# A two-block transformer kernel on one core: the modulation rows, x's first norm and the load order at its beginning

## The chip, the core and the metric

One core of a Trainium2 chip runs the whole program. Its engines are TensorE (PE in the rows, its weight loads PEld), VectorE (DVE), ScalarE (ACT) and GpSimd (POOL); SyncE (SP) issues nearly all loads. The metric is the device time of one execution in microseconds. The kernel before takes 1417.83 us (median of 3 runs, 1417.08 to 1421.2).

## The reference

The input is one sequence of 256 tokens, 1024 wide. Two layers with adaptive norms are followed by a third layer; each has several FFNs and mixers. What concerns the change is the very beginning, layer 0's first FFN, and the long filter that layer 1 needs:

```python
cond = jax.nn.silu(c)
m = (cond @ w_mod[l] + b_mod[l]).reshape(bsz, 3, 3, D_MODEL)      # 9 sections of 1024
def adaln_in(x, g, m, i):
    return rmsnorm(x, g) * (1 + m[:, i, 1][:, None]) + m[:, i, 0][:, None]
def swiglu(h, w1, w3, w2):
    return (jax.nn.silu(h @ w1) * (h @ w3)) @ w2                    # 2752 wide inside
x = x + 0.5 * m[:, 0, 2][:, None] * swiglu(adaln_in(x, norm_g[l, 0], m, 0), ...)

# hyena_filter: three sine layers on 33 features of 256 positions, then 64 -> 2 x 512
h = jnp.sin(fq * (z @ w1 + b1))     # three of these, then
h = (h @ w4).reshape(L, 2, CONV_WIDTH) * decay
```

So before FFN 0 can start, `silu(c)` must meet 1024 x 2048 numbers of `w_mod` (the scale section and the shift section), and x must be squared and summed.

## The kernel before, in words

Everything is kept transposed: features on the 128 partitions, the 256 tokens along the free axis. Each weight tile is 128 x 1024 in float32 (512 KB). ScalarE rounds it to a high part (`hi_job`, L584), VectorE subtracts to get the low part (`lo_job`, L595), and each product is three one-pass matmuls: high by high, high by low, low by high (`mm3`). An FFN's first half is 43 slabs of 8 such blocks, so 24 matmuls a slab; `slab_mms` (L678) takes the first three slabs together, and three PSUM tiles (`mmr`, `u_127` to `u_129` in the order) hold them. The second half follows in `block_mms`.

All loads go through one list (`order`, L549): `m` tiles of `w_mod`, `w` tiles of weights. SyncE issues them in that order into a ring of six raw tiles (`raws`, `u_75` to `u_80`); a tile comes free when its last reader has run, and an issue that waits holds up all behind it. `RATES` says how many `m` tiles follow each `w` tile; `extra` and `EX` put the small loads (x, the filter's tables, vectors) ahead of a given entry.

Modulation is made in two ways. An `m` tile of the usual kind holds 128 outputs on the partitions and 1024 inputs along the free axis: one VectorE multiply-and-sum (`tensor_tensor_reduce` against `condb`, the row `silu(c)` copied to all partitions) gives 128 outputs. For the groups of four tiles named in `PE_GROUPS` (L133) the tiles are stored the other way round and `pe_mod` (L630) makes 512 outputs as a row on TensorE: eight float32 matmuls with a one-column stationary operand `c` and 512 moving columns each, then a ScalarE copy and four small matmuls that turn the row into columns. Before, only group 2 goes this way. Groups 0 and 1 are the scale section, 2 and 3 the shift section.

FFN 0 is the only one whose norm is applied before its matmuls (`nm.whole`): ScalarE squares the eight blocks of x, GpSimd adds them, TensorE sums over partitions, VectorE makes the inverse root, `spread` makes a tile of it, and `normalise` (L818) multiplies x by the gain and by it, in one VectorE instruction a block, and splits the result. The shift is carried as two more columns of the operand (258 instead of 256, `shift_cols`), and comes back out of PSUM as a bias that ScalarE copies before each silu. Beside this `hyena_spectrum` (L1528) makes the filter; `reduce_angle` brings its angles into range with GpSimd and VectorE in turn; its last layer adds and subtracts the two halves of `w4` on GpSimd, `tap_sums` squares and adds on ScalarE and GpSimd.

The program is written by generators under a planner (`Sched`, L330): each job says which engine it wants next, and the one with the earliest modelled start plus a penalty is emitted. On the chip each engine then runs its list strictly in that order. All engine calls pass through one helper, so nearly every row of the profile has line L442.

Of the kernel before, what the change touches and what calls it, by code (L numbers as in the profile page):

```python
# [20 lines left out]
P = 128  # L21
# [111 lines left out]
PE_GROUPS = (2,)  # L133
# [4 lines left out]
def _pack(inp):  # L138
# [135 lines left out]
    out["fw4"] = np.ascontiguousarray(inp["d_f_w4"][0])  # L274
# [18 lines left out]
EX = (2, 3, 8)  # L293
DRATE, DLAT = 350.0, 1.3
HPEN = -0.6
# [5 lines left out]
RATES = [(43, 0.55), (65, 0.7), (91, 0.5), (156, 0.31), (199, 0.5), (221, 0.75), (247, 0.4), (10 ** 6, 0.2)]  # L301
# [28 lines left out]
class Sched:  # L330
# [61 lines left out]
    def charge(self, e, cost, early=0.0, cols=0.0):  # L392
# [19 lines left out]
        if e == "pe":  # L412
            self.debt = 0.0 if j.main else self.debt + cost

# [59 lines left out]
def _body(tc, ins, out, ctx, dbg=None):  # L474
# [74 lines left out]
    order = [("m", i) for i in range(12)] + [("w", 0)] + [("m", i) for i in range(12, 16)]  # L549
    mi, credit = 16, 0.0  # L550
    for i in range(NW):
        if i:
            order.append(("w", i))
# [8 lines left out]
    m_ev = {(l, s): Event() for l in range(2) for s in range(9)}  # L562
    cond_ev, x_ev = Event(), Event()
# [31 lines left out]
    def lo_job():  # L595
        for oi, (kind, i) in enumerate(order):
# [13 lines left out]
            else:  # L610
# [8 lines left out]
                mod_done(l, M_SECS[r // 8], 1)  # L619
# [4 lines left out]
    def mod_done(l, s, n):  # L624
        m_left[l, s] = m_left.get((l, s), 8) - n
        if m_left[l, s] == 0:
            fire(m_ev[l, s])


    def pe_mod(g, ccol, one1, row):  # L630
# [3 lines left out]
        for i in range(4):  # L634
            oi = order.index(("m", 4 * g + i))
            yield raw_ev[oi]
# [4 lines left out]
            put(raws, raw_t.pop(oi))  # L641
        yield "act"
        act.activation(row, b[0:1], AF.Copy)
# [3 lines left out]
        for j in range(4):  # L647
            pe.matmul(b[:, j:j + 1], row[:, j * P:j * P + P], one1[:, 0:1], start=True, stop=True)
# [3 lines left out]
        mod_done(0, M_SECS[g // 2], 4)  # L652
# [140 lines left out]
    class Norm:  # L793
        def __init__(self, A, h, lo, width=D):
# [5 lines left out]
            self.adder = ("dve", dve)  # L800
# [17 lines left out]
        def normalise(self, k, src):  # L818
            yield self.done
            t, = yield sc, 1  # L820
            yield "dve"
            dve.scalar_tensor_tensor(t, src, self.A[:, k:k + 1], self.rstd, ALU.mult, ALU.mult)
            yield from split(self.h[:, k, :T], self.lo[:, k, :T], t, self.need(k))
            put(sc, t)
            self.use()
# [7 lines left out]
        def square(self, src):  # L833
# [110 lines left out]
    def ffn(l, i, nm, nxt):  # L944
        with tc.tile_pool(name=f"ffn{l}{i}", bufs=1) as sp:
# [5 lines left out]

            def done(s, ps):
                t, = yield sc, 1
                b, = yield sm, 1
                if nm.whole:
                    h = ps[:, :T]
                    yield "act"
                    act.activation(b[:, 0:1], ps[:, T:T + 1], AF.Copy)
                else:
                    h = t  # L960
                    yield from evict(nm, t, b[:, 0:1], ps)
                j = s // 2
                if s == 42:
# [4 lines left out]
                    if nm.whole:  # L968
                        put(mmr, ps)
# [5 lines left out]
                elif s % 2 == 0:  # L975
                    yield "act"
                    act.activation(t, h, AF.Silu, bias=b[:, 0:1])
                    if nm.whole:
                        put(mmr, ps)
# [4 lines left out]
                else:  # L984
# [3 lines left out]
                    if nm.whole:  # L988
                        put(mmr, ps)
# [5 lines left out]
            if not nm.whole:  # L995
# [509 lines left out]
    def reduce_angle(a, shift):  # L1505
        t, = yield sc, 1
        n = t[:a.shape[0], :a.shape[1]]
        yield "pool"
        if shift:
            pool.tensor_scalar(n, a, 1.0 / TWO_PI, shift / TWO_PI, ALU.mult, ALU.add)  # L1510
            pool.tensor_scalar(n, n, MAGIC, None, ALU.add)
        else:
            pool.tensor_scalar(n, a, 1.0 / TWO_PI, MAGIC, ALU.mult, ALU.add)
        yield "pool"
        pool.tensor_scalar(n, n, -MAGIC, None, ALU.add)
# [12 lines left out]
    def hyena_spectrum(sp, small, fw4, dec, df, small_ev, big_ev):  # L1528
# [26 lines left out]
        w4 = tl(sp, [64, 2, 512])  # L1555
        yield "pool"
        pool.tensor_tensor(w4[:, 0], fw4[:, :512], fw4[:, 512:], ALU.add)
        pool.tensor_tensor(w4[:, 1], fw4[:, :512], fw4[:, 512:], ALU.subtract)
        for tt in range(2):
            for half in range(2):  # L1560
                b, = yield chb, 1
                yield "pe"
                pe.matmul(b, hcur[:, tok(tt)], w4[:, half], start=True, stop=True)
# [3 lines left out]
            if tt == 0:  # L1567
                k0 = kf[0:1, :, 0]
                yield "pool"
                pool.tensor_tensor(k0[:, 0], k0[:, 0], k0[:, 1], ALU.add)  # L1570
                pool.tensor_scalar(k0[:, 0], k0[:, 0], 0.5, None, ALU.mult)
                pool.tensor_copy(k0[:, 1], k0[:, 0])
        put(sc, *hs)
        sums = spawn(tap_sums(kf, sq))
# [22 lines left out]
    def tap_sums(kf, sq):  # L1597
        for i in range(4):
# [3 lines left out]
            if i:  # L1602
                yield "pool"
                pool.tensor_tensor(sq[0], sq[0], sq[1], ALU.add)
# [593 lines left out]
    def main():  # L2198
        small_ev, big_ev, c_ev = Event(), Event(), Event()
        with tc.tile_pool(name="start", bufs=1) as sp:  # L2200
            w4, dec, df = tl(sp, [64, D]), tl(sp, [P, 2, 512]), tl(sp, [P, 2, 512])
            crow, one1 = tl(sp, [8, D]), tl(sp, [1, P])
# [3 lines left out]
            load(crow[0:1], ins["c"], 4)  # L2206
            load(vec0, ins["vec"][:, :NVEC0], NVEC0 / 2, c_ev)
            load(small, ins["small"], 115, small_ev)
            extra[EX[0]] = [(mat0, ins["mat"][:, :2 * P], 131)]
# [119 lines left out]
```

## Time and profile before

| what | value |
|---|---|
| median of 3 runs | 1417.83 us |
| profiled execution, its own time | 1418.68 us |
| its span, first to last instruction | 1416.7 us |
| TensorE busy in the span | 1366.5 us (96%), weight loads 1281.4 us (90%) |
| VectorE, ScalarE, GpSimd busy | 1143.4 us, 782.4 us, 38.1 us |
| moved from memory | 302.37 MB read, 214 GB/s over the span |

The engines run side by side, so busy times are not added. In the 40 slices of the page TensorE stands at nine tenths or more nearly everywhere, except in the first slice of 35 us (5 tenths) and the second (8 tenths). GpSimd is busy in the first two slices and hardly after.

### The profile page before, as it was taken

The numbers are of one execution on the slowest core, as the hardware profiler recorded it, in microseconds if no ns is written. First come the engines' busy times: TensorE is split into PE (matmuls) and PEld (weight loads), VectorE is DVE, ScalarE is ACT, GpSimd is POOL, SyncE is SP. The second block draws the span as 40 slices with busy tenths as digits, with TensorE's granted clock in tenths as the row PEclk, the third lists the DMA queues.
The fourth block names the chain that finished last, engine by engine and source line by source line (L and its number), as shares of the span: only waits on it lengthen the run. The fifth ranks groups of instructions, "written<-read, shape, count | busy, mean of one in ns | idle before, by whom it ended". The sixth has DMA issues, their size and how long they took to land.

```text
span 1416.7 us, 27169 instructions
## 1 busy us (share of the span) xinstructions
PE 1366.5 (96%) x10830; PEld 1281.4 (90%) x10830; DVE 1143.4 (81%) x2183; ACT 782.4 (55%) x1440; POOL 38.1 (3%) x42
## 2 busy tenths in 40 slices
PE   5899999998999999999999999999999999999998
PEld 1499999878999999999998789999996779899998
DVE  5788788787888777888979889986578958799962
ACT  2365554374555544555446646655458656676642
POOL 5200000000000000000000001000000000000000
PEclk9999999999999999999999999999998999999999
DMA  8679889845877777988984447675643225366671
GB/s 296 223 257 310 291 308 330 259 135 174 251 259 246 242 244 226 300 274 273 344 299 149 150 156 231 223 256 181 193 149 120 88 80 160 97 187 182 192 232 51
DMA packets 84593, 305.20 MB, mean 215 GB/s; under 512 B 9476, under 2 KB 11108, under 8 KB 84211
## 3 DMA queue, kind: packets, MB, share of 16 engines
q1 hardware_dynamic: 83250, 299.31, 65.0%
q0 software_dynamic: 1216, 4.16, 0.9%
q8 instruction: 85, 1.39, 0.4%
q14 instruction: 42, 0.34, 0.1%
HBM read 302.37 MB, written 1.06 MB: 214 GB/s over the span
## 4 chain that ended last, share of the span: by engine, by line
PE 83%; DVE 8%; ACT 6%; DMA 1%; issue 1%; POOL 1%; SPq 0%; ACTq 0%; DVEq 0%; POOLq 0%
PE u L442 83%; DVE u L442 8%; ACT u L442 5%; POOL u L442 1%; DMA u<-wst 1%; DMA u<-mst 1%; ACT L442 0%; SPq L569 0%; POOL u L2135 0%; ACTq L442 0%; DVEq L442 0%; DVE u L1634 0%; DVE u L1144 0%; DVE u L1635 0%; DVEq L1144 0%
## 5 line engine op out<-in xcount | busy, mean ns | idle before, releaser
L442 PE MATMUL u<-u,u 128*128 128x256 f32 (+6 forms) x10828 | 1365.5, 292 | 46.4 <-ACT u L442 26.2
L442 PEld LDWEIGHTS u<-u,u 128*128 128x128 f32 (+4 forms) x10828 | 1281.1, 188 | 129.8 <-issue 54.0
L442 ACT ACTIVATE u<-u 128x1024 fp32r<-128x1024 f32 (+5 forms) x999 | 602.4, 632 | 537.9 <-PE u L442 309.1
L442 DVE TENSOR_TENSOR u<-u,u 128x1024 fp32r<-128x1024 f32 (+6 forms) x1065 | 733.7, 720 | 177.4 <-ACT u L442 91.7
L442 DVE SCALAR_TENSOR_TENSOR u<-u,u,u 128x256 f32<-128x256 f32 (+2 forms) x393 | 185.3, 481 | 57.0 <-PE u L442 28.8
L442 ACT ACTIVATE u<-u,u 128x256 f32<-128x256 f32 (+3 forms) x331 | 169.7, 521 | 68.6 <-DVE u L442 56.6
L442 DVE CUSTOM_DVE_ANT_0 u<-u,u,u 128x1024 f32<-128x1024 f32 x140 | 180.8, 1293 | 3.9 <-ACT u L442 3.5
L442 DVE SCALAR_TENSOR_TENSOR u<-u,u 128x2 f32<-128x2 f32 (+5 forms) x127 | 32.9, 262 | 8.3 <-POOL u L442 5.3
L442 ACT ACTIVATE u<-u,u,u 128x256 f32<-128x256 f32 (+1 forms) x43 | 23.8, 564 | 10.1 <-DVE u L442 7.5
L442 DVE TENSOR_SCALAR u<-u,u 128x256 f32<-128x256 f32 (+1 forms) x80 | 25.7, 371 | 2.4 <-ACT u L442 1.6
L442 DVE TENSOR_SCALAR u<-u 128x2 f32<-128x2 f32 (+9 forms) x82 | 15.1, 186 | 7.9 <-PE u L442 4.2
L442 DVE TENSOR_REDUCE u<-u 128x2 f32<-128x512 f32 x20 | 13.2, 683 | 4.3 <-PE u L442 4.3
L442 ACT ACT_TABLE_LOAD x11 | 14.1, 1283 | 0.9 <-PEq L2306 0.7
L442 POOL TENSOR_TENSOR u<-u,u 128x256 f32<-128x256 f32 (+1 forms) x10 | 13.1, 1308 | 13.6 <-ACT u L442 13.2
L1319 POOL DMA_DIRECT2D u<-rope x1 | 0.6, 551 | 478.6 <-PE u L442 478.6
L442 POOL TENSOR_SCALAR u<-u 64x256 f32<-64x256 f32 (+2 forms) x12 | 12.3, 1027 | 24.5 <-DVE u L442 18.3
L442 DVE DVE_READ_ACCUMULATOR2_ANT u<- 128x1 f32 x156 | 12.8, 82 | 0.0
L442 ACT ACTIVATION_READ_ACCUMULATOR u<-u,u,u 128x1 f32 x40 | 8.2, 204 | 0.0
L442 DVE TENSOR_TENSOR u<-u 128x2 f32<-128x2 f32 (+5 forms) x36 | 6.8, 188 | 0.7
L442 DVE CUSTOM_DVE_ANT_0 u<-u,u 128x256 f32<-128x256 f32 x16 | 6.0, 421 | 1.6 <-PE u L442 1.6
L1141 POOL DMA_DIRECT2D u<-sink x1 | 0.6, 642 | 192.5 <-DMA u<-mst 192.5
L442 DVE RECIPROCAL u<-u 128x4 f32<-128x4 f32 (+2 forms) x17 | 3.0, 174 | 3.5 <-ACT u L442 3.3
(33 smaller groups left out, 27.2 us busy)
## 6 DMA issues: line engine op xcount, KB each, us to landing
u<-wst SPq DMA_DIRECT2D x417, 512.0 KB, 4.5
u<-mst SPq DMA_DIRECT2D x144, 512.0 KB, 4.8
u<-u POOLq DMA_DIRECT2D x1, 1536.0 KB, 12.1
u<-x SPq DMA_DIRECT2D x1, 1024.0 KB, 8.4
u<-mem SPq DMA_DIRECT2D x1, 1024.0 KB
u<-lruw POOLq DMA_DIRECT2D x2, 512.0 KB, 4.4
out<-u SPq DMA_DIRECT2D x8, 128.0 KB, 2.6
u<-decay SPq DMA_DIRECT2D x1, 512.0 KB, 9.2
```

Source lines behind the costliest of these rows:

```text
L442: r = f(*args, **kw)
L1141: nc.gpsimd.dma_start(snk, bass.AP(ins["sink"].tensor, ins["sink"].offset, [[0, P], [1, 16]]))
L1319: nc.gpsimd.dma_start(rope, ins["rope"])
```

## The change

The scale section (groups 0 and 1) is made on TensorE too, and `pe_mod` now works in strips: the stationary operand `cz` is a block of 32 columns of which the first is `silu(c)`, four such blocks stand side by side in the 128 columns of the array, and each takes another 128 inputs; two rounds of four matmuls replace eight. The row has its four partial sums on four partitions, and the turn into columns adds them. x's squares are added on VectorE. `normalise` multiplies by the inverse root on VectorE first, as soon as that is known, and applies gain and shift together on ScalarE later, so that FFN 0 has 256 columns and no bias (`done_whole`). The angles of both users of `reduce_angle` are on VectorE. The filter's `w4` is stored with its halves on top of each other, and three ScalarE copies make the two stationary operands instead. The loads stand in another order: x and the filter's tables earlier, `w` 0 to 2 between `m` 9 to 11, and 0.6 `m` tiles a weight in FFN 0 instead of 0.55. Penalties put the beginning's jobs first.

```diff
-PE_GROUPS = (2,)
+PE_GROUPS = (0, 1, 2)
-EX = (2, 3, 8)
+EX = (0, 1, 4)
-RATES = [(43, 0.55), (65, 0.7), ...
+RATES = [(43, 0.6), (65, 0.7), ...
-    order = [("m", i) for i in range(12)] + [("w", 0)] + [("m", i) for i in range(12, 16)]
+    order = [("m", i) for i in range(9)]
+    for i in range(3):
+        order += [("w", i), ("m", 9 + i)]
+    order += [("m", i) for i in range(12, 16)]
...
+    def pe_mod(g, cz, row):
...
+        for i in (0, 2):
+            ts = []
+            for j in range(2):
+                oi = order.index(("m", 4 * g + i + j))
+                yield raw_ev[oi]
+                ts.append(raw_t.pop(oi))
             yield "pe"
-            for e in range(2):
-                k = 2 * i + e
-                pe.matmul(b[0:1], ccol[:, k:k + 1], raw_t[oi][:, 512 * e:512 * e + 512], start=(k == 0), stop=(k == 7))
+            for q in range(4):
+                pe.matmul(b[32 * q:32 * q + 32], cz[:, 2 * i + q], ts[q // 2][:, q % 2 * 512:q % 2 * 512 + 512],
+                          start=(i == 0), stop=(i == 2), tile_position=(0, 32 * q))
+            put(raws, *ts)
         yield "act"
-        act.activation(row, b[0:1], AF.Copy)
+        act.activation(row, b, AF.Copy)
...
-        def normalise(self, k, src):
+        def normalise(self, k, src, gain, shift, ev):
             yield self.done
             t, = yield sc, 1
             yield "dve"
-            dve.scalar_tensor_tensor(t, src, self.A[:, k:k + 1], self.rstd, ALU.mult, ALU.mult)
+            dve.tensor_tensor(t, src, self.rstd, ALU.mult)
+            self.use()
+            yield gain
+            yield ev
+            yield "act"
+            act.activation(t, t, AF.Identity, scale=self.A[:, k:k + 1], bias=shift)
             yield from split(self.h[:, k, :T], self.lo[:, k, :T], t, self.need(k))
...
-                yield self.adder[0]
-                self.adder[1].tensor_tensor(self.acc, self.acc, s, ALU.add)
+                yield "dve"
+                dve.tensor_tensor(self.acc, self.acc, s, ALU.add)
...
+            if nm.whole:
+                yield from slab_mms(43, xh, xl, T, done_whole, nm.kev(), parts=[(k,) for k in range(8)])
+            else:
...
-            yield from shift_mod(l, 2 * i)
-            yield from slab_mms(43, xh, xl, T + 2, done, nm.kev())
+                yield from shift_mod(l, 2 * i)
+                yield from slab_mms(43, xh, xl, T + 2, done, nm.kev())
...
-                act.activation(ccol, ccol, AF.Silu)
+                act.activation(cz[:, :, 0], ccol, AF.Silu)
```

The lists below are what the planner emitted. In all, `u_75` to `u_80` are the raw tiles and `u_134`, `u_130` to `u_133` small PSUM tiles. First TensorE, from the sum of squares (`u_93`) to the last row that is turned into columns; `u_63` holds `silu(c)` as columns, `u_247` the filter's `w4`. Before:

```order
L442 MATMUL u_133<-u_65,u_93 128x1 x2
L442 MATMUL u_134<-u_77,u_63 1x512 x2
L442 MATMUL u_130<-u_247,u_91 128x512
L442 MATMUL u_132<-u_65,u_104 128x128 x2
L442 MATMUL u_131<-u_247,u_91 128x512
L442 MATMUL u_134<-u_78,u_63 1x512 x2
L442 MATMUL u_134<-u_79,u_63 1x512 x2
```

After, where `u_151` is the block of strips, `u_152` and `u_153` the first two rows, `u_104` the inverse root:

```order
L446 MATMUL u_133<-u_65,u_93 128x1 x2
L446 MATMUL u_134<-u_75,u_151 32x512 x2
L446 MATMUL u_134<-u_76,u_151 32x512 x2
L446 MATMUL u_134<-u_77,u_151 32x512 x2
L446 MATMUL u_134<-u_78,u_151 32x512 x2
L446 MATMUL u_133<-u_92,u_155 64x256
L446 MATMUL u_132<-u_65,u_104 128x128 x2
L446 MATMUL u_134<-u_65,u_152 128x1 x4
L446 MATMUL u_130<-u_79,u_151 32x512 x2
```

The first group's matmuls now stand ahead of the filter's third layer and of the spreading of the inverse root; the second group follows at once.

Next the last group and the start of FFN 0 on TensorE after the change; `u_177` is the filter in time, `u_148` the transform, `u_68` and `u_69` the high and low parts of FFN 0's operand, `u_81` to `u_86` of the weights:

```order
L446 MATMUL u_131<-u_75,u_151 32x512 x2
L446 MATMUL u_131<-u_77,u_151 32x512 x2
L446 MATMUL u_132<-u_177,u_148 128x512
L446 MATMUL u_134<-u_65,u_154 128x1 x4
L446 MATMUL u_130<-u_177,u_148 128x512 x2
L446 MATMUL u_133<-u_177,u_148 128x512 x2
L446 MATMUL u_127<-u_68,u_81 128x256
L446 MATMUL u_127<-u_69,u_81 128x256
L446 MATMUL u_127<-u_68,u_82 128x256
L446 MATMUL u_131<-u_177,u_148 128x512 x2
L446 MATMUL u_128<-u_68,u_83 128x256
```

Two pairs of the filter's transform (one is the `128x512 x2` shown last, the other a `1x512 x2`) stand inside the first block of FFN 0, which now goes block by block over all three slabs.

Last ScalarE after the change, from the squares of x (`u_67`) to the block of strips (`u_151`); `u_142` is `condb`:

```order
L446 ACTIVATE u_99<-u_67 128x256
L446 ACTIVATE u_100<-u_67 128x256
L446 ACTIVATE u_92<-u_134,u_103,u_63 64x256
L446 ACT_TABLE_LOAD
L446 ACTIVATE u_142<-u_130 128x512
L446 ACTIVATE u_142<-u_131 128x512
L446 ACTIVATE u_151<-u_63 128x8
```

Before, `silu(c)` was made first on ScalarE and the squares came after it; now `silu(c)` stands behind the squares, a layer of the filter and a table load.

## Rows read from the trace of the kernel before

**Rows 1.** windows: stretch, length, busy (instructions) by engine, clock, DMA share, GB/s

```profile
0.00:62.00 62.00, 40.13 (x76) 12.06 (x77) 46.59 (x79) 22.69 (x45) 27.29 (x29) 0.95 0.76 263
72.00:150.00 78.00, 78.00 (x655) 78.00 (x655) 64.46 (x90) 44.12 (x85) 0.00 (x0) 1.00 0.86 292
190.00:240.00 50.00, 50.00 (x427) 50.00 (x426) 43.80 (x62) 23.48 (x31) 0.00 (x0) 1.00 0.92 319
1250.00:1300.00 50.00, 50.00 (x431) 50.00 (x430) 47.95 (x91) 34.60 (x55) 0.00 (x0) 1.00 0.63 189
```

**Rows 2.** chain that ended last, first 75 us: start, us, what

```profile
30.97 13.86 PE u L442 x24
...
46.80 10.64 DVE u L442 x15
...
57.48 13.27 PE u L442 x77
```

**Rows 3.** timeline, first 72 us: start, us, engine, instruction, idle before

```profile
12.62 1.03 ACT L442 ACTIVATE u<-u 128x256 f32<-128x256 f32 x3 [1.05 <-DMA u<-x]
...
17.66 7.61 POOL L442 TENSOR_TENSOR u<-u,u 128x256 f32<-128x256 f32 x5
...
71.50 0.65 PEld L442 LDWEIGHTS u<-u,u 128*128 128x128 f32 x5 [0.26 <-ACT u L442]
```

**Rows 4.** the timeline of TensorE's weight loads, 25 to 62 us

```profile
36.91 0.13 PEld L442 LDWEIGHTS u<-u,u 128*1 128x1 f32 x1 [0.72 <-issue]
...
39.02 0.08 PEld L442 LDWEIGHTS u<-u,u 128*1 128x1 f32 x1 [0.34 <-issue]
```

**Rows 5.** windows, TensorE alone, granted clock after the busy count

```profile
56.00:58.00 2.00, 0.52 (x2) 0.50 0.84 304
...
62.00:64.00 2.00, 2.00 (x17) 0.89 0.92 346
```

**Rows 6.** groups by form, TensorE: 1066-1068, 1074-1076, 1080-1082 us

```profile
L442 PE MATMUL u<-u,u 64*64 64x256 f32 x8 | 0.7, 402 | 0.0
...
L442 PE MATMUL u<-u,u 64*64 64x256 f32 x8 | 1.1, 658 | 0.0
...
L442 PE MATMUL u<-u,u 128*32 128x128 f32 x16 | 0.6, 278 | 0.0
```

**Rows 7.** windows, TensorE alone, one period of the gates

```profile
1074.48:1076.48 2.00, 2.00 (x12) 0.50 0.01 4
```

**Rows 8.** groups by form, first 75 us: busy us, mean ns | idle

```profile
L442 DVE CUSTOM_DVE_ANT_0 u<-u,u,u 128x1024 f32<-128x1024 f32 x14 | 19.6, 1421 | 3.9 <-ACT u L442 3.5 <-DMA u<-mst 0.4
...
L442 PE MATMUL u<-u,u 128*1 128x512 f32 x20 | 13.8, 838 | 0.0
...
L442 POOL TENSOR_TENSOR u<-u,u 128x256 f32<-128x256 f32 x7 | 8.7, 1249 | 4.3 <-ACT u L442 4.0
...
L442 ACT ACTIVATE u<-u 128x512 f32<-128x512 f32 x11 | 6.4, 602 | 4.9 <-PE u L442 3.6 <-POOL u L442 1.2
...
L442 ACT ACTIVATE u<-u 128x256 fp32r<-128x256 f32 x9 | 3.6, 417 | 6.1 <-DVE u L442 6.1
...
L442 DVE TENSOR_TENSOR u<-u,u 128x256 fp32r<-128x256 f32 x9 | 3.3, 419 | 0.5 <-ACT u L442 0.5
...
L442 ACT ACTIVATE u<-u,u,u 64x256 f32<-64x256 f32 x3 | 1.7, 557 | 1.6 <-PE u L442 1.6
...
L442 ACT ACT_TABLE_LOAD x1 | 1.3, 1283 | 0.7 <-PEq L2306 0.7
```

**Rows 9.** DMA view, first 75 us: 38 slices; KB each, us to landing

```profile
GB/s 2 171 284 342 418 404 411 417 422 288 232 389 419 413 417 98 0 103 409 48 4 105 402 339 166 356 31 208 208 303 313 273 277 332 417 361 20 0 0 0
...
u<-mst SPq DMA_DIRECT2D x20, 512.0 KB, 6.0
```

**Rows 10.** page, section 6, whole run: KB each, median us to landing

```profile
u<-wst SPq DMA_DIRECT2D x417, 512.0 KB, 4.5
u<-mst SPq DMA_DIRECT2D x144, 512.0 KB, 4.8
```

More of the change, by code (lines that the diff above doesn't have):

```diff
@@ L562, in _body @@
     m_ev = {(l, s): Event() for l in range(2) for s in range(9)}
+    slab_ev = [Event() for _ in range(16)]
     cond_ev, x_ev = Event(), Event()
@@ L618, in lo_job, with mod_done @@
                     op0=ALU.mult, op1=ALU.add, accum_out=mods[l][:, c:c + 1])
-                mod_done(l, M_SECS[r // 8], 1)
+                mod_done(i)
             put(raws, raw_t.pop(oi))
     m_left = {}
[L624 to L630, printed above, removed]
+    def mod_done(i):
+        key = i // 72, M_SECS[i % 72 // 8]
+        m_left[key] = m_left.get(key, 8) - 1
+        if i < 16:
+            fire(slab_ev[i])
+        if m_left[key] == 0:
+            fire(m_ev[key])
+    def pe_mod(g, cz, row):
         c0 = M_SECS[g // 2] * 8 + g % 2 * 4
@@ L647, in pe_mod @@
         for j in range(4):
-            pe.matmul(b[:, j:j + 1], row[:, j * P:j * P + P], one1[:, 0:1], start=True, stop=True)
+            pe.matmul(b[:, j:j + 1], row[:, j * P:j * P + P], ones[:, 0:1], start=True, stop=True)
         yield "dve"
@@ L651, in pe_mod @@
         put(chb, b)
-        mod_done(0, M_SECS[g // 2], 4)
+        for i in range(4):
+            mod_done(4 * g + i)
     def tune(name):
@@ L949, in ffn, with done_whole @@
             sl = {}
+            def done_whole(s, ps):
+                t, = yield sc, 1
+                h = ps[:, :T]
+                j = s // 2
+                if s == 42:
+                    h3, = yield sc, 1
+                    yield "act"
+                    act.activation(h3[:64], h[64:], AF.Copy)
+                    act.activation(t[:64], h[:64], AF.Silu)
+                    put(mmr, ps)
+                    yield "dve"
+                    dve.tensor_tensor(t[:64], t[:64], h3[:64], ALU.mult)
+                    put(sc, h3)
+                    yield from split(gh[:64, j], gh[64:, j], t[:64], kev[j])
+                elif s % 2 == 0:
+                    yield "act"
+                    act.activation(t, h, AF.Silu)
+                    put(mmr, ps)
+                    sl[j] = t
+                    fire(st[j])
+                    return
+                else:
+                    yield st[j]
+                    yield "dve"
+                    dve.tensor_tensor(t, h, sl[j], ALU.mult)
+                    put(mmr, ps)
+                    put(sc, sl.pop(j))
+                    yield from split(gh[:, j], gl[:, j], t, kev[j])
+                put(sc, t)
             def done(s, ps):
@@ L954, in done @@
                 b, = yield sm, 1
[L955 to L961, printed above, removed]
+                h = t
+                yield from evict(nm, t, b[:, 0:1], ps)
                 j = s // 2
@@ L1554, in hyena_spectrum @@
         yield big_ev
[L1555 to L1558, printed above, removed]
+        hsum, hdif = hs
+        yield "act"
+        act.activation(hsum[64:], hsum[:64], AF.Copy)
+        act.activation(hdif[:64], hsum[:64], AF.Copy)
+        act.activation(hdif[64:], hsum[:64], AF.Copy, scale=-1.0)
         for tt in range(2):
@@ L1562, in hyena_spectrum @@
                 yield "pe"
-                pe.matmul(b, hcur[:, tok(tt)], w4[:, half], start=True, stop=True)
+                pe.matmul(b, hs[half][:, tok(tt)], fw4, start=True, stop=True)
                 yield "dve"
@@ L2228, in main @@
             spawn(cond())
-            for g in PE_GROUPS:
-                spawn(pe_mod(g, ccol, one1, crow[0:1, 512:]))
+            for g, row in zip(PE_GROUPS, rows):
+                spawn(pe_mod(g, cz, row), -1.0)
             spawn(hi_job(), urgency(0))
@@ L2237, in first @@
                 nm = box[0]
-                nm.adder, nm.whole = ("pool", pool), True
+                nm.whole, nm.uses = True, 8
                 yield x_ev
                 for k in range(8):
-                    spawn(nm.square(x[:, k]))
+                    spawn(nm.square(x[:, k]), -1.0)
+                ready = Event()
+                js = [spawn(nm.normalise(k, x[:, k], ready, mods[0][:, k:k + 1], slab_ev[8 + k]), -0.5) for k in range(8)]
                 a = (yield from gain_mod(0, 0))
                 nm.A = a.A
-                nm.uses = 8
-                for j in [spawn(nm.normalise(k, x[:, k])) for k in range(8)]:
+                fire(ready)
+                for j in js:
                     yield j.end
                 put(sm, a.A)
-            spawn(first())
+            spawn(first(), -1.0)
             nm = box[0]
```

67 lines of the change are left out of this document (31 added, 36 removed).

## The prediction

> **What bounds the kernel now.** I read the windows by stage first. From 72 us on TensorE is busy in every microsecond of the long stretches; up to 62 us it is busy for 40 of 62, VectorE for 47 and GpSimd for 27 [rows 1]. So the end of the program is TensorE's work plus what TensorE waits, and the change touches the one place where it waits long. The chain shows the order there: TensorE with small float32 matmuls, then 10.6 us of VectorE alone, then FFN 0's matmuls [rows 2]. The timeline gives the marks: x is there at 12.62; its squares are added on GpSimd, the last five from 17.66 to 25.3; the fourth slab of FFN 0 begins at 71.50 [rows 3]. That last mark is my measure: three slabs done, TensorE steady from there on.
>
> Two clock levels matter. Two weight loads of the same kind of matmul are 0.72 us and later 0.34 us of idle apart, with 0.13 and 0.08 of load [rows 4]: half a float32 matmul of 512 columns takes 0.85 us early and 0.43 from 39 us on, so a whole one 1.71 or 0.86. These are the 1.2 and 2.4 GHz levels, as the granted clock shows later: after TensorE had stopped for some microseconds it stood at 0.50, and was back at 1.00 during 62 to 64, some 5 us after work resumed [rows 5].
>
> **Strips, the part on which most hangs.** Before, eight matmuls with one stationary column make a row; 20 records, two to a matmul, are busy 13.8 us [rows 8]. Now four stand in strips of 32 columns. Do four run at once? Four matmuls of 64x64 tiles, 256 columns, in two row and two column halves: eight records took 0.7 us in one place and 1.1 us in another [rows 6], where one alone would take 0.43 or 0.85; in sequence they would need 1.7 and 3.4. Eight matmuls with 32-column strips and 128 columns took 0.6 us in 16 records [rows 6]; in sequence at the high level 1.7. So I take one round of four at one matmul's time plus 0.2 to 0.3: 1.05 us (high level) or 2.0 (low), six rounds in all. In sequence a round would take 3.4 or 6.8; that is the other end.
>
> A cost beside it: a period of 2.00 us at granted clock 0.50 holds one such round of four and three main matmuls of 256 columns [rows 7]; 2.00 - 0.85 - 3 x 0.215 leaves 0.5 us for one change into tiles and one out of them, 0.25 each at the low level. The new order has eight changes (in and out, four times). I charge 1.3 us, two at 0.25 and six at half of it; bounds 0 and 2. The Trainium skill, "TensorEngine Tiling (Array Packing)", Key Properties, says that a change of tiling mode drains TensorE, which speaks against the change; this trace agrees with a price of a quarter of a microsecond, and a drain of a full matmul each would make the sum some 5 us worse.
>
> **The new beginning, step by step** (us from the span's start).
> 1. x. Two `m` tiles fewer lie ahead of it. In the fifth to ninth of 38 slices the loads moved 404 to 422 GB/s [rows 9], so 1.05 MB less is 2.55 us: x at 10.1 instead of 12.6.
> 2. ScalarE: eight squares at 0.345 (three took 1.03 [rows 3]) to 12.85, the filter's layer 0.56, a table load 1.28, two `condb` halves at 0.60, `cz` 0.2 [rows 8]: 16.1. VectorE adds squares meanwhile at about 0.42 instead of GpSimd's 1.25 [rows 8], done near 13.9.
> 3. TensorE: group 0 was loaded long before; two rounds at the low level, 4.0: 20.2. Then the filter's third layer, the spread of the inverse root and the turn of the row, about 1.1, 1.2 and 1.5: 24.0. By then it has worked 8 us on end, about as long as it took before (31 to 39 us), so from here I take the high level.
> 4. Group 1. Its last two tiles reuse raw tiles that group 0 frees at 18.4, and land near 23.5: two rounds, 26.0.
> 5. Group 2. The raw tile of `m` 9 is free at 25.0; the trace's loads take 4.5 to 4.8 us over the whole run [rows 10] and 6.0 in the crowded beginning [rows 9]; I take 4.7 here. `m` 11 needs the tile that `m` 8 leaves, near 31.0 (the filter's copies on ScalarE and two 512-column matmuls stand before it), so it lands at 35.7 and its round ends at 36.7. This chain of three tiles, each waiting for TensorE to read another, now paces the beginning, where 14 multiply-and-sums on VectorE (19.6 us [rows 8]) did before; four of those are left before FFN 0's start.
> 6. The row's copy 0.6, a transform matmul 0.86 and the turn 1.1, then on VectorE a multiply-and-sum of 1.35 that stands ahead, and the bias: 39.4.
> 7. ScalarE from there: eight scale-and-shift copies at 0.56, eight high parts at 0.42, three filter copies at 0.6 [rows 8], in the emitted order. Block 0's high part is the tenth: 43.5, its low part 0.42 later: 43.9. The last block follows at 49.3.
> 8. TensorE: 72 matmuls at 0.117 (8.4) and, inside block 0, two pairs of 512 columns (3.45): 43.9 + 11.9 = 55.8; the blocks are ready before they are wanted. With the 1.3 of mode changes: 57.1.
>
> So the mark moves from 71.5 to 57.1: 14.4 us.
>
> **The rest.** FFN 0's slabs lose two columns. In the long stretches 655 matmuls of 258 columns take 78 us, 119.1 ns each; 427 of 256 take 50 us, 117.1, and 431 in the last FFN 116.0 [rows 1]. For the remaining 40 slabs of 24: 960 x 2.0 ns = 1.9 us, up to 3.0. The 43 ScalarE bias copies that go lie beside TensorE: nothing. The stream of FFN 0 grows from 0.55 to 0.6 `m` tiles a weight: 0.05 x 1.35 us more on VectorE a slab of 2.8, where it is 83% busy (64.46 of 78 [rows 1]), and 1.6 x 0.524 MB in 2.8 us, 300 GB/s where 400 were moved: nothing, if VectorE keeps up. The angles of the last tables move from GpSimd to VectorE beside FFN matmuls: nothing. Later lists differ in short runs of the mixers, where the planner's times fell otherwise; I take 0, bounds -2 and +2.
>
> Sum, against the profiled execution's 1418.68 (the median is 0.9 lower): 14.4 + 1.9 = 16.3 less, **1402 us**.
>
> **The rivals.**
> - The low level stays. Between 24 and 44 us TensorE waits several times for tiles, and waiting took the clock down before [rows 5]. Then the matmuls on step 4 to 6's path cost about 5 us more and the first half of block-by-block work some 2 more: mark at 64, total 1409. For it: the level held low from 2 to 39 us before, with work in between. Against: steps 3 and 4 are denser than anything before 31 us then. 0.18.
> - Loads as slow as the beginning's median, 6.0 instead of 4.7 on three tiles in a row: 4 us, 1406. 0.11.
> - Better: tiles and high level come sooner, the mixers' new order helps by 2: 1396. 0.07.
> - No net gain: VectorE, 83% busy, cannot follow the earlier and denser stream, and TensorE stalls in FFN 0 until the 16 us are spent: about 1417. Against it: in the same stretch it was never late for TensorE (78.00 of 78 busy [rows 1]), and its load grows by 0.07 us a slab only. 0.05.
> - Slower: strips do not run at once in float32 with all 128 rows in use and the level stays low. Place: the three groups of `pe_mod`. Price: 24 matmuls at 1.71 are 41 us, where I count six rounds for 8.2; with the other small matmuls at the low level the mark comes near 95, total about 1440. It decides against the change from 24.5 us for the 24, 1.0 us each; at the high level (0.86) it would eat the gain and no more. Against it: the 16 records in 0.6 us [rows 6]. 0.03. The skill's "TensorE: Matmul & The Clock Gate", Part 3, gives 2.38 times for three column strips of 512; by that figure a round of four would take about 1.3 us at the high level (an estimate from that page), 2 us more over the six.
>
> **How the numbers follow.** The forecast has 0.56, with its own spread of 4 us. Faster by over 0.3% (4.3 us, what a measurement of this kernel can tell): forecast, low level, slow loads, better: 0.92. Within 0.3%: 0.05. Slower: 0.03. The range reaches from the better case's far side, 1394, to just past the low level's, 1411; what is left out is the last two rivals and some tails.
>
> **What would show it.** In the changed profile: groups of four 32-column matmuls start within some tens of nanoseconds (strips); x's squares begin near 10 us; `m` 11 lands near 36; FFN 0's first 256-column matmul stands near 44 and the fourth slab's first weight load near 57; weight loads of 512-column matmuls 0.43 apart from 24 us on (0.85 means the first rival). From there on TensorE should be full, with 117 ns a matmul in FFN 0. I am wrong if the mark lies past 66, or if it lies near 57 and the total is still over 1410: then something later gave it back.

## The result and the profile after

| | before | after |
|---|---|---|
| median | 1417.83 us (5 runs, 1417.03 to 1421.2) | 1408.46 us (5 runs, 1399.61 to 1412.38) |
| profiled execution: span | 1416.7 us | 1406.7 us |
| first slab of FFN 0 read by ScalarE | 70.77 us | 58.78 us |

The ratio on record is 0.9899, with an interval of 0.9874 to 0.9924: faster by about 1%. The two medians of the table alone give 0.9934, 9.4 us. The forecast was 1402 us with a range of 1394 to 1411. Eight more executions of the changed kernel came with the experiments; over all 13 the median is 1405.35 us. The kernel before was measured 40 times more beside the experiments, with medians of 1419.37, 1420.12 and 1421.98 us and times from 1416.75 to 1426.56. It spreads over 10 us, then, not over 4, and beside these executions the changed kernel gains 14 us or more (1405.15 against 1419.37 in `again`).

The mark below is the start of ScalarE's first read of a slab (70.77 before, 58.78 after). The fourth slab's first weight load, which the prediction used, stands 0.7 us behind it before and 0.4 us behind it after (71.50 and 59.22). The page's part on busy time, engine by engine, and then the stretches of [rows 1] in the changed kernel (busy us and records of PE, PEld, DVE, ACT, POOL, then granted clock, DMA share, GB/s):

```profile
PE 1367.5 (97%) x10878; PEld 1283.6 (91%) x10878; DVE 1133.9 (81%) x2193; ACT 783.2 (56%) x1411; POOL 7.1 (1%) x16
```

```profile
0.00:62.00 62.00, 52.92 (x215) 27.09 (x216) 36.33 (x84) 33.69 (x64) 2.43 (x8) 0.94 0.79 288
72.00:150.00 78.00, 78.00 (x671) 78.00 (x671) 65.91 (x93) 38.77 (x57) 0.00 (x0) 1.00 0.91 317
1250.00:1300.00 50.00, 50.00 (x431) 50.00 (x430) 47.45 (x90) 33.79 (x54) 0.00 (x0) 1.00 0.58 189
```

In the first 62 us TensorE is busy for 52.9 instead of 40. FFN 0 runs 671 matmuls in 78 us, 116.2 ns each, where it ran 655. VectorE has nearly the same load there as before (65.91 us for 64.46) and TensorE never waits. The chain of waits of the changed kernel, in order of time, answers to [rows 2]:

```profile
3.17 6.76 DMA u<-x
9.96 3.01 ACT u L446 x9
12.98 1.28 ACT L446
14.28 1.20 ACT u L446 x3
...
15.52 15.44 PE u L446 x66
30.96 5.59 DMA u<-mst
...
36.60 7.75 PE u L446 x18
44.37 1.89 ACT u L446 x4
...
46.28 0.77 DVE u L446 x2
...
47.10 23.01 PE u L446 x170
```

The 10.6 us of VectorE alone are gone. TensorE's work up to 30.96 frees a raw tile, `m` 11 takes 5.59 us to come into it, and the rest hangs on that. The timeline shows the start of the same stretch, VectorE's adds beside ScalarE's squares, and the strips' weight loads (answering to [rows 3, 4]):

```profile
9.96 2.56 ACT L446 ACTIVATE u<-u 128x256 f32<-128x256 f32 x8 [0.75 <-DMA u<-x]
10.71 3.61 DVE L446 TENSOR_TENSOR u<-u,u 128x256 f32<-128x256 f32 x7 [1.96 <-ACT u L446]
...
15.52 0.20 PEld L446 LDWEIGHTS u<-u,u 128*32 128x32 f32 x8 [0.21 <-ACT u L446]
16.37 0.20 PEld L446 LDWEIGHTS u<-u,u 128*32 128x32 f32 x4 [0.66 <-issue]
17.22 0.20 PEld L446 LDWEIGHTS u<-u,u 128*32 128x32 f32 x4 [0.66 <-issue]
```

Four strips stand in each group of loads, and the groups are 0.85 us apart: half a round of four takes what half of a single 512-column matmul took early [rows 4]. Last, the granted clock around the wait for `m` 11 (PE's busy time alone):

```profile
38.00:40.00 2.00, 2.00 (x8) 0.51 1.05 358
40.00:42.00 2.00, 2.00 (x6) 0.50 0.91 354
42.00:44.00 2.00, 2.00 (x3) 0.50 1.00 401
44.00:46.00 2.00, 2.00 (x5) 0.78 0.95 356
46.00:48.00 2.00, 1.68 (x6) 1.00 0.72 287
```

After a wait of 1.91 us the engine stood at the low level (1.2 GHz) from 38 to 45 us, in the middle of the first transforms. The granted clock shows this fall, but not the low level at the very start: it reads 1.00 in every window from 12 to 34 us, also where the weight loads are 0.85 us apart. The first rise is therefore read from the weight loads.

Where the 10.0 us between the two profiled spans come from, by places that both traces have (the starts of the same matmuls after the same waits). "Low" is the sum of (1 - granted clock) x time in steps of 5 us:

| stretch | before | after | difference | of it low |
|---|---|---|---|---|
| to the first slab's read | 70.77 | 58.78 | -12.0 | |
| to FFN 0's end (248.44; 234.28) | 177.67 | 175.50 | -2.2 | 0 |
| to layer 0's last mixer matmuls (329.26; 315.12) | 80.82 | 80.84 | 0.0 | 0 |
| to 541.57; 529.28 | 212.31 | 214.16 | +1.85 | +1.7 |
| to layer 1's last mixers (823.83; 811.55) | 282.26 | 282.27 | 0.0 | 0 |
| to 1037.06; 1028.64 | 213.23 | 217.09 | +3.9 | +1.7 |
| to the third layer's last mixers (1204.09; 1194.17) | 167.03 | 165.53 | -1.5 | -1.7 |
| to the end | 212.61 | 212.53 | -0.1 | -1.7 |

### The profile page after: what moved, and what is told of

Same layout as the page of the kernel before. It is cut to its first block, busy times and chain, and to the rows that moved or that the text cites. A ratio compares the mean times of both kernels' runs of the same rounds, so it can differ in the third digit from the quotient of the medians.

```text
span 1406.7 us, 27283 instructions
## 1 busy us (share of the span) xinstructions
PE 1367.5 (97%) x10878; PEld 1283.6 (91%) x10878; DVE 1133.9 (81%) x2193; ACT 783.2 (56%) x1411; POOL 7.1 (1%) x16
## 4 chain that ended last, share of the span: by engine, by line
PE 84%; DVE 7%; ACT 6%; DMA 2%; issue 1%; SPq 0%; ACTq 0%; DVEq 0%
PE u L446 84%; DVE u L446 7%; ACT u L446 5%; DMA u<-mem 1%; DMA u<-x 0%; DMA u<-mst 0%; ACT L446 0%; DMA u<-wst 0%; SPq L578 0%; ACTq L446 0%; DVEq L446 0%; DVE u L1680 0%; DVE u L1681 0%; DVEq L1188 0%; DVE u L1682 0%
## 5 line engine op out<-in xcount | busy, mean ns | idle before, releaser
L446 PEld LDWEIGHTS u<-u,u 128*128 128x128 f32 (+2 forms) x10876 | 1283.3, 188 | 114.8 <-issue 45.6
L446 DVE TENSOR_TENSOR u<-u,u 128x256 f32<-128x256 f32 (+6 forms) x1105 | 751.4, 709 | 191.3 <-ACT u L446 99.2
L446 ACT ACTIVATE u<-u 128x1024 fp32r<-128x1024 f32 (+6 forms) x983 | 605.3, 646 | 516.9 <-PE u L446 310.9
L446 DVE SCALAR_TENSOR_TENSOR u<-u,u,u 128x256 f32<-128x256 f32 (+2 forms) x364 | 169.9, 476 | 47.9 <-PE u L446 30.1
L446 ACT ACTIVATE u<-u,u 128x256 f32<-128x256 f32 (+3 forms) x308 | 158.4, 524 | 75.0 <-DVE u L446 61.9
L446 DVE CUSTOM_DVE_ANT_0 u<-u,u,u 128x1024 f32<-128x1024 f32 x132 | 168.5, 1277 | 1.0 <-DMA u<-mst 0.9
L446 ACT ACTIVATE u<-u,u,u 128x256 f32<-128x256 f32 (+1 forms) x51 | 28.4, 568 | 11.9 <-DVE u L446 8.9
L446 DVE TENSOR_SCALAR u<-u 128x8 f32<-128x8 f32 (+10 forms) x94 | 18.2, 194 | 12.8 <-ACT u L446 6.4
L446 DVE TENSOR_TENSOR u<-u 128x2 f32<-128x2 f32 (+6 forms) x37 | 7.5, 202 | 0.8
L446 DVE TENSOR_TENSOR_SCAN u<-u,u 128x256 f32<-128x256 f32 x8 | 5.4, 680 | 0.0
(30 smaller groups left out, 12.6 us busy)
```

The costliest lines, as they stand in the source:

```text
L446: r = f(*args, **kw)
```

## The experiments

**again: the changed kernel once more.** No edit.

> The changed kernel once more, for a second profile and its spread: five runs so far lie between 1399.6 and 1412.4 us, where the kernel before stays within 4 us. Theory A (given back in the mixers by the new order of the lists): the first three slabs end near 59 us in every run, and the mixers of layers 0 and 1 lose the same 5 us again; the time is 1405 to 1411. Rival B (the low clock comes and goes): a profile with another total shows low-clock stretches in other places, near 350 and 815 us above all, and the total moves with their sum.

Measured: 1405.15 us (6 runs, 1401.41 to 1411.65), ratio 0.9898 (0.9869 to 0.9927). Its profile differs from the first though the lists are the same: the first slab is read at 52.98, nothing falls in the beginning, and later it has 20.5 us of low clock where the first profile had 8.5. The span was 1409.8. Theory A (59 us in every run) fails; rival B is borne out: beside falls near 345 and 805 us, as in the first profile, there are others near 830 and 1120, and the longer total goes with their sum, not with the beginning.

**again2, again3: two more executions.** No edit.

> The changed kernel once more, for one look. Its first two profiles read the first slab of FFN 0 at 58.8 us (m 11 late, clock fallen) and at 53.0 (not). Theory that this wait decides between two beginnings and that its executions differ by it: again one of these two, with the weight loads 0.85 us apart before the first slab where it is 58 to 59, and 0.43 where it is 53. Rival, that the beginning is always one of the two and the other profile an exception by chance of the clock alone: a third value, with m 11's wait the same as in one of the two.

> As the run before it, a second look at the same kernel: 53 or 58 to 59 us for the first slab, by whether TensorE waits over 1.5 us for m 11.

Measured: 1402.82 and 1405.35 us, first slab at 52.81 and 55.40. So there are not two beginnings but three, and the theory of the expectation of again2 falls. The weight loads tell them apart. Of again2, from the strips of group 0 on, then m 11's round:

```profile
17.11 0.20 PEld L446 LDWEIGHTS u<-u,u 128*32 128x32 f32 x4 [0.66 <-issue]
18.77 0.19 PEld L446 LDWEIGHTS u<-u,u 64*64 64x64 f32 x2 [1.46 <-issue]
...
21.23 0.12 PEld L446 LDWEIGHTS u<-u,u 128*32 128x32 f32 x2 [0.30 <-issue]
21.66 0.12 PEld L446 LDWEIGHTS u<-u,u 128*32 128x32 f32 x2 [0.31 <-issue]
...
33.63 0.14 PEld L446 LDWEIGHTS u<-u,u 128*32 128x32 f32 x4 [1.12 <-DMA u<-mst]
34.62 0.30 PEld L446 LDWEIGHTS u<-u,u 128*128 128x128 f32 x2 [0.84 <-issue]
```

Of again3, the same places:

```profile
17.12 0.20 PEld L446 LDWEIGHTS u<-u,u 128*32 128x32 f32 x4 [0.66 <-issue]
18.98 0.29 PEld L446 LDWEIGHTS u<-u,u 64*64 64x64 f32 x2 [1.66 <-issue]
...
23.52 0.20 PEld L446 LDWEIGHTS u<-u,u 128*32 128x32 f32 x4 [0.66 <-issue]
24.38 0.20 PEld L446 LDWEIGHTS u<-u,u 128*32 128x32 f32 x4 [0.66 <-issue]
```

In again2 the high level (2.4 GHz) begins near 19 us: half a round is 0.43 us from then on. In again3, as in the first profile, half rounds still take 0.86 at 24 us, and 0.43 only from about 28 on. `m` 11's tile is freed at 28.46 in the one and at 31.02 in the other, by the chains of waits, and its load lands 5.1 us later, at 33.59 and 36.19. That is the 2.6 us between them. again3 waits 1.48 us for it and keeps its clock; the first profile waits 1.91 and loses it. That makes the 3.4 us from 55.4 to 58.8: 0.4 is the later load (the round starts at 36.60 instead of 36.23), and 3.0 go with the fall, whose low-clock sum is 3.4 (0.95 + 2.45 in two 5-us steps). One pair of profiles does not make the length of the wait the cause of the fall; below, waits of 1.8 us are found with a fall and without one.

**warm: idle matmuls while TensorE waits for m 11.** Group 2's second round got five more matmuls between its two tiles, the identity by a constant tile, into PSUM that nobody reads.

```diff
...
+                if q == 2 and fill is not None:
+                    for _ in range(5):
+                        nc.tensor.matmul(fill[:, :2 * P], ident, mat0, start=True, stop=True)
...
```

> Five idle float32 matmuls (identity, 256 columns, result unused) stand where TensorE waits for the last tile of group 2 (34.7 to 36.6 us); all lists are otherwise the same. Theory: the low clock from 38 to 45 us comes from that wait and costs about 3.5 us; with the wait filled the weight loads at 41 to 44 us stand 0.43 apart instead of 0.85, the first slab ends near 55.5 instead of 58.8, and the total is 3 us lower. Rival: the clock falls for the low activity of the strips before it, wait or no wait; then nothing moves.

Measured: 1409.11 us (7 runs, 1403.58 to 1415.11), ratio 0.993 (0.9902 to 0.9958), span 1406.6. The beginning has no fall and the first slab is at 53.84, but this execution had the high level from 19 us anyway, so it would not have waited long; later it has 15.4 us of low clock. Its median lies 4 us above that of `again`, and the two intervals overlap: no gain of 3 us shows. What the fall in the beginning costs was thus not tested here, because the execution profiled had none to prevent.

**seq: the strips one after another.** All matmuls of `pe_mod` use the same 32 columns, so that none run side by side.

```diff
-                pe.matmul(b[32 * q:32 * q + 32], ..., start=(i == 0), stop=(i == 2), tile_position=(0, 32 * q))
+                pe.matmul(b[:32], ..., start=(i == 0 and q == 0), stop=(i == 2 and q == 3), tile_position=(0, 0))
...
```

> The same stationary blocks of 32 columns, but all four of a round in the same strip, one after another, summed in PSUM. Theory (strips do run at once): each round costs three matmuls of 512 columns more, 5.1 us at the low and 2.6 at the high level; six rounds, of which the last two hide partly behind loads: the first slab ends 12 to 20 us later than 58.8, which gives the whole gain back; total 1418 to 1428. Rival (the gain comes from VectorE's relief and the load order, and strips matter little): under 4 us later.

Measured: 1422.28 us (10 runs), ratio 1.0014 (0.9997 to 1.0031), first slab at 65.54. TensorE is now the bound of the beginning:

```profile
14.93 37.88 PE L446 MATMUL u<-u,u 128*128 128x1 f32 x102 [3.24 <-DVE u L446]
53.37 16.85 PE L446 MATMUL u<-u,u 128*128 128x256 f32 x114 [0.56 <-ACT u L446]
```

In the total, strips that do not run at once take back the whole gain. At the mark they take back 7 to 13 us of it (65.54 against 58.78 and 52.81), less than the 12 to 20 expected, and 65.54 is still 5.2 us sooner than before. The price is less than the 41 us of the slower rival because the high level came at 20 us: the weight loads stand 0.43 apart from there, 0.86 to a matmul. The rest lies later, where its profile has 18.8 us of low clock; that this comes of the strips is not shown.

**mfirst: m 9 to 11 ahead of w 0 to 2.** Only the load order is changed.

```diff
-    order = [("m", i) for i in range(9)]
-    for i in range(3):
-        order += [("w", i), ("m", 9 + i)]
+    order = [("m", i) for i in range(12)] + [("w", i) for i in range(3)]
```

> Tiles m 9 to 11 stand ahead of weights 0 to 2 in the load order, so that m 11 finds a free raw tile at once. Theory (three loads in a row, each waiting for TensorE to free a tile, pace the beginning): no wait of 2 us for m 11, the shift row is done some 5 us sooner, the clock does not fall, and the first slab ends at 53 to 55, if the weights (now later) do not take over; total 1402 to 1406. Rival: the weights' high and low parts become the last to arrive, and the first slab ends no sooner than 58.

> The version with m 9 to 11 loaded ahead of w 0 to 2 once more, as the base of the three others of this round: 1401 us (its four times lay from 1400.1 to 1402.3), first slab of FFN 0 read near 53.3 us. If its small spread then was chance, its times spread as those of the changed kernel, 1400 to 1412, because the low clock in the mixers falls differently in each execution.

Measured: 1401.18 (4 runs) and 1402.11 us (5 runs), ratios 0.9863 (0.9838 to 0.9888) and 0.9868 (0.9847 to 0.989). All nine lie between 1400.07 and 1404.07, where the changed kernel's lie over 12.8 us. The first slab is at 53.32 (high level from 28 us) and 51.47 (from 19): a late rise, with a first round that starts 1.15 us later, costs 1.9 us here and no fall follows. Taking the wait for `m` 11 out of the beginning is worth about 4 us at the median (3.2 to 4.2). Why these nine spread so little is not shown: the long execution profiled in `again` had an early first slab and lost its time later, and g2 and fill, with the same load order as here, spread over 12 and 7 us again.

**g2: the scale section back on VectorE**, in mfirst's order.

```diff
-PE_GROUPS = (0, 1, 2)
+PE_GROUPS = (2,)
```

> The version with m 9 to 11 first, but the scale section (groups 0 and 1) back on VectorE, 8 multiply-and-sums more of 1.35 us there and four rounds of strips fewer. Theory of the prediction, that these multiply-and-sums paced the beginning: FFN 0's first slab is read 7 to 11 us later (60 to 64 instead of 53), 1408 to 1412 us. Rival, that VectorE has time for them while the loads arrive (8 tiles at 0.5 MB need 10 us at 400 GB/s, about what they cost) and that TensorE gains by the rounds left out: 51 to 55, 1399 to 1403 us.

Measured: 1405.94 us (6 runs, 1399.82 to 1411.6), ratio 0.9889 (0.9864 to 0.9914), first slab at 54.03. The multiply-and-sums start at 16.56 us and run while the loads come in; only the last stands behind the wave of 33.64 in VectorE's timeline:

```profile
33.64 3.37 DVE L446 TENSOR_TENSOR u<-u,u 128x256 f32<-128x256 f32 x9 [0.28 <-ACT u L446]
36.93 1.27 DVE L446 CUSTOM_DVE_ANT_0 u<-u,u,u 128x1024 f32<-128x1024 f32 x1
```

So in the beginning the move of 1024 outputs to TensorE is worth 0.7 to 2.6 us (54.03 against 53.32 and 51.47), not the 7 to 11 that the theory asked for. Of these, up to 1.7 are low clock: this profile has a fall at 29 to 33 us, behind waits of 4.28, 1.00 and 0.80 us. At the median it is 3.8 us beside mfirst2's 1402.11, within what the two intervals leave open.

**poolnorm: the squares of x added on GpSimd again**, in mfirst's order.

```diff
-                yield "dve"
-                dve.tensor_tensor(self.acc, self.acc, s, ALU.add)
+                e = ("pool", pool) if self.whole else ("dve", dve)
+                yield e[0]
+                e[1].tensor_tensor(self.acc, self.acc, s, ALU.add)
```

> The version with m 9 to 11 first, but the squares of x added on GpSimd again (seven adds of 1.25 us instead of 0.42 on VectorE). Theory that the chain of m tiles through TensorE sets the beginning, and that the norm is hidden: adds end near 20 instead of 14, the spread of the inverse root follows group 0's strips anyway, first slab read at 53 to 55, 1401 to 1403 us. Rival, that the norm is on the path, since spread and turn stand ahead of group 1 on TensorE: all 6 us come through, 59, 1407 us.

> The version with the adds of x's squares on GpSimd once more, for one look: its first profile read the first slab at 53.5 us, in line with a hidden norm, but its six times lay 6 us above those of the version without that edit. If the norm is nevertheless on the path, and the first profile was the lucky one (it was the fastest of the six), the first slab is read at 57 to 59 here; if not, at 53 to 54, and the 6 us lie in the mixers behind it.

Measured: 1408.27 us (6 runs, 1405.99 to 1411.36), ratio 0.9911 (0.9891 to 0.993), and 1408.91 once more. First slab at 53.46 and 54.31, so that the beginning agrees with a hidden norm. But the premise was off, as GpSimd's row shows, and below it a piece of the chain of waits of the kernel before:

```profile
10.78 5.65 POOL L446 TENSOR_TENSOR u<-u,u 128x256 f32<-128x256 f32 x7 [8.30 <-ACT u L446]
```

```profile
20.21 4.26 POOL u L442
```

Seven adds take 5.65 us here, 0.72 to 0.79 each. The 1.25 us of [rows 8] are a mean over seven adds of which one took 4.26 us, beginning at 20.21 as VectorE began three multiply-and-sums end to end (to 23.89); the other six took 0.72 to 0.80 before too. Why the one was slow was not tried. In poolnorm VectorE runs none there, and the adds end at 16.4, only 2.1 us behind VectorE's. Of the 6 us of the total some 1.5 are in the beginning and 2.5 in low clock (13.65 and 13.6 us in the two profiles, against 11.95 and 10.35); the other 2 these profiles do not place. The expected 1401 to 1403 us was missed.

**fill, fill2: idle matmuls in the mixers**, in mfirst's order. Before the matmuls that waited 0.5 to 2.3 us, TensorE multiplies the identity by itself into PSUM that nobody reads; the lists are the same otherwise.

```diff
+            if self.name == "pe":
+                self.k = self.k + 1 if "k" in self.__dict__ else 0
+                for _ in range(FILL.get(self.k, 0)):
...
+                    self.eng.matmul(b[:, 3 * P:], ident, ident, start=True, stop=True)
...
+FILL = {2148: 5, 2416: 6, 6033: 4, 6197: 4, 8748: 4}
```

This is fill2's list, 23 idle matmuls in five places; fill has 46 in ten.

> The same version, with 46 idle matmuls (128 columns of the identity by itself, 0.22 us each at the high level, into PSUM columns that nobody reads; nothing of the result changes) put on TensorE in front of ten matmuls of the mixers that waited 0.5 to 2.3 us for ScalarE or VectorE. Theory that the clock falls because TensorE waits there: the low-clock sum after the first slab goes from 12 us to 4 or less, and the median from 1401 to about 1393. Rival, that the level falls for what TensorE runs there (matmuls of 1, 8 or 128 columns): the sum stays at 10 to 20 us, and the time at 1401 to 1405.

> The version with m 9 to 11 first, with 23 idle matmuls in five places of the mixers (of the 46 in ten places before, those left out that themselves waited for a PSUM tile). Theory, that the clock falls where TensorE waits: no fall at 306, 345, 805, 830 and 1190 us, a low-clock sum after the first slab of 3 to 6 us instead of 10 to 12, and 1396 to 1400 us. Rival, that the idle matmuls cost as much as they save, as 46 did: 1401 to 1405.

Measured: fill 1404.64 us (6 runs), ratio 0.9891 (0.9868 to 0.9913), low clock after the first slab 5.1 us; fill2 1398.82 us (6 runs, 1398.18 to 1403.36), ratio 0.9849 (0.9822 to 0.9875). At one filled place, mfirst2 and mfirst, both without idle matmuls, and mfirst2's clock of 805 to 810 us:

```profile
805.75 24.31 PE L446 MATMUL u<-u,u 128*128 128x256 f32 x172 [1.77 <-ACT u L446]
```

```profile
806.62 22.66 PE L446 MATMUL u<-u,u 128*128 128x256 f32 x172 [1.76 <-ACT u L446]
```

```profile
805.00:810.00 5.00, 4.18 (x14) 0.69 0.51 184
```

fill2, with its eight records of idle matmuls (L453), and the same clock:

```profile
800.97 1.05 PE L453 MATMUL u<-u 128*128 128x128 f32 x8
802.91 22.67 PE L454 MATMUL u<-u,u 128*128 128x256 f32 x172 [0.88 <-ACT u L454]
```

```profile
805.00:810.00 5.00, 5.00 (x35) 1.00 0.04 16
```

The same 172 records take 22.67 us in fill2, 24.31 in mfirst2 behind a fall, and 22.66 in mfirst, behind the same wait, without a fall and without idle matmuls. So this place shows what a fall costs, 1.65 us, but not that the idle matmuls prevent it: of the twelve profiles without them in the mixers only six have a fall here, and the kernel before has none (22.66 us behind a wait of 1.77).

Two other places say more. Near 1060 and 1190 us all twelve profiles have a fall, and fill, which fills both, has none at either. Yet in fill2 the clock falls at 1185 us, from inside the idle matmuls put there. The mean clock of whole executions points the same way as fill: 0.990 to 0.996 in fill and 0.993 to 0.996 in fill2, against 0.989 to 0.993 in the nine executions of mfirst and mfirst2. So the clock falls behind TensorE's waits, in some executions and not in others, and with them filled falls were rarer; the rival of fill's expectation, that the work itself brings the fall, is not excluded by one profile each.

For the total of fill that expectation's theory failed (1404.64 us, not 1393): at 1052 and 1057 us the idle matmuls themselves waited 2.26 and 1.49 us for ScalarE, and 10 us of added work ate the 5 to 7 us won. fill2 leaves those two places and three others out. Its time came as expected (1396 to 1400 us), its low clock did not: its profile has 10.2 us where 3 to 6 were expected, 6.8 of it at 1045 to 1065, where it fills nothing, as much as mfirst2's 10.35. So the 2.8 us between these two spans are not low clock, and where they lie is open. fill2 has the best median of all and is 1.5% faster than the kernel before; against the changed kernel the intervals just touch, against mfirst they overlap.

## Why the prediction was right, and where it was off

The direction and the mechanism held: the time came out of the beginning, by x and the norm earlier, strips that run at once, and a chain of three `m` tiles that paces what is left. Of these seq tests the strips, mfirst the chain and poolnorm a part of the norm; x's earlier load and `normalise` in two steps were not taken back by themselves. By its own steps:

- **Steps 1 and 2** (x at 10.1, `cz` at 16.1): 9.96 and 15.47. That GpSimd's adds took 1.25 us each was a misreading of a mean (see poolnorm), but the step counts only VectorE's 0.42, and they were done at 14.3 instead of 13.9.
- **The strips**: 1.05 and 2.0 us a round were taken, 0.86 and 1.71 measured. The 1.3 us charged for changes of mode come out about right. In the first profile, around one round:

```profile
28.02 1.08 PEld L446 LDWEIGHTS u<-u,u 128*128 128x128 f32 x9 [0.32 <-issue]
29.86 0.16 PEld L446 LDWEIGHTS u<-u,u 128*32 128x32 f32 x8 [0.76 <-issue]
30.86 0.30 PEld L446 LDWEIGHTS u<-u,u 128*128 128x128 f32 x2 [0.84 <-issue]
31.40 0.19 PEld L446 LDWEIGHTS u<-u,u 128*128 128x128 f32 x1 [0.24 <-DVE u L446]
```

  From the last load ahead of the round (28.91: 28.02 + 1.08 less its own 0.19) to the load of 31.40 TensorE ran five halves of 512 columns, 2.14 us at 0.43 each; it took 2.48. So a change in and a change out cost 0.34 us together at the high level, as they do in mfirst (2.91 us for six halves, from 29.82 to 32.73), and four such pairs 1.4 (an estimate; where TensorE waits anyway, part of it is hidden). From the first FFN 0 matmul to the fourth slab's weight load it takes 12.6 us, 46.61 to 59.22, against 11.9 in step 8. The Trainium skill's "TensorE: Matmul & The Clock Gate", Part 3, gives 2.38 times for three strips; here four strips take one matmul's time. By that figure a round of four would come to about 1.2 us (an estimate), not the prediction's 1.3.
- **Steps 3 to 5** (high level from 24.0, `m` 11's tile freed at 31.0, landed at 35.7): mis-sized, and not one number. The level rose at 19 or at 28 us, never at 24; the tile was freed at 28.5 or 31.0, landed at 33.6 to 33.8 or 36.2 to 36.6. The load took 5.1 to 5.6 us, between the 4.7 taken and the 6.0 of the second rival. When the wait for it was 1.9 us, the first rival came in part: a fall that cost 3.0 us. The predicted mark of 57.1, about 56.5 at the first slab's read, lies among the four measured, 52.8, 53.0, 55.4 and 58.8. That is partly luck: a rise at 24 us lies between the two that occur, and the load was taken 0.4 to 0.9 us too short.
- **Step 5's reason, that 14 multiply-and-sums on VectorE paced the beginning before**: g2 gives eight of them back and loses 0.7 to 2.6 us there. They did not pace it by their length. What ended the 10.6 us of VectorE alone [rows 2] is to be sought among the other parts, x and the norm earlier, `normalise` in two steps, group 2 in two rounds; how it divides over these was not tried.
- **Columns**: 1.9 (up to 3.0) was taken; mark to FFN 0's end shrank by 2.2 us.
- **"The rest 0, bounds -2 and +2"** is the term that failed: in the pair of profiled executions it is +4.1, by the table, and makes most of the 6.5 us between forecast and median. TensorE waits longer where layer 1's third FFN begins: before, three matmuls in a row there waited 0.48, 0.54 and 0.44; after,

```profile
837.09 0.39 PE L446 MATMUL u<-u,u 128*128 128x258 f32 x1 [1.22 <-ACT u L446]
838.54 9.70 PE L446 MATMUL u<-u,u 128*128 128x258 f32 x79 [1.06 <-DVE u L446]
849.59 2.65 PE L446 MATMUL u<-u,u 128*128 128x258 f32 x20 [1.35 <-ACT u L446]
```

that is 2.2 us. The planner's new order there is the likeliest reason; it was not tried. Another 1.6 come behind 1194 us, at the third layer's last mixers, once the low clock is set aside. And the low clock after the mark is no constant: 8.5, 20.5, 8.5 and 8.6 us in four executions of the same lists. I had set it equal before and after. In the pair of profiled executions it happens to be (8.5 each), but it goes with the spread: of the runs of the changed kernel the fastest (1399.6 and 1401.4) have a mean clock of 0.996, the slowest four (1409.6 to 1412.4) 0.985 to 0.989.

Span less mark and less low clock is 1334.6 to 1339.8 us in all twelve profiles without idle matmuls in the mixers, before's 1337.4 among them. So FFN 0's 2.2 us are given back by the waits, and within these 5 us no other change behind the beginning can be told. Open is why the level first rises at 19 us in one execution and at 28 in the next, and why again3 has 3.45 us of low clock at 740 to 750 us, where no wait is recorded.

## What to carry to other kernels

A gain at the start of a long program is measured at a mark (the first steady work), and the rest is compared stretch by stretch between places that both traces have; only so are 2 us of new waits told from 2 us of clock. Where loads, tiles and the engine's own speed form a ring (tile read, freed, loaded, read), forecast a range of times for it and put first in the queue what the critical engine needs first: here that was worth about 4 us at the median. A wait of 1 to 2 us on TensorE costs more than itself when the clock falls behind it, which it did in some executions and not in others, so one profile with and one without a measure do not show what it does. A mean over a few instructions can hide a single long one, so look at each before the mean goes into a sum.

## What was not expected of the hardware

- Four float32 matmuls in strips of 32 columns by 512 take the time of one: 0.86 us at the high level, 1.71 at the low. A change into strips and out again adds 0.34 us at the high level.
- With the same lists and first rounds within 0.3 us of each other (15.2 to 15.5) TensorE's clock first rose at 19 us (again, again2) or at 28 (the first profile, again3).
- One fall of the clock has a low-clock sum of about 1.7 us or twice that (1.45 + 0.25 at 350 us, 1.05 + 0.65 at 810, 0.95 + 2.45 at 35 to 45). The same wait of 1.8 us ended with a fall at 805 us in mfirst2 and without one in mfirst.
- Of seven GpSimd adds of 128x256 one took 4.26 us, while VectorE ran multiply-and-sums; the other six took 0.72 to 0.80.
